# An attention kernel with its softmax maxima taken in pairs, the second layer's first scores moved in front of its values, and the output projections begun in front of the last head's values

## The chip, the cores and the metric

The kernel runs on one core of a Trainium2 chip. The metric is the device time of one execution in microseconds, as the median of several runs. TensorE (PE) multiplies, VectorE (DVE), ScalarE (ACT) and GpSimd (POOL) do the elementwise work, SyncE (SP) issues the loads of weights. Each engine has its own list of instructions, in an order that is fixed when the program is built, and works it off from the top; an instruction may wait on a semaphore for work of another engine, and what stands behind it on that engine waits as well.

## The reference

A diffusion backbone of two layers on 256 latent and 256 context tokens of width 1024, all in f32. Each layer is a half-step SwiGLU block, a token mixer and a second half-step SwiGLU block, each on a normalised and modulated input. The mixer of layer 0 is multi-head latent attention (MLA, 8 heads), for latent and context tokens; that of layer 1 is windowed attention (SWA, 16 query heads on 4 key heads) with a sink logit per head, for the latent tokens alone. In the SWA the latent keys and queries are rotated, the context ones aren't, and one softmax runs over the window, the context and the sink:

```
s_w = jnp.einsum('bkgqd,bkjd->bkgqj', q_rot, k_b).astype(jnp.float32) * scale
s_w = jnp.where(valid, s_w, NEG_INF)
s_c = ctx_scores(q_pl)
...
p_w, p_c, _ = joint_softmax(s_w, s_c, s_s)
return pv('bkgqj,bkjd->bkgqd', p_w, v_b) + pv('bkgqc,bkcd->bkgqd', p_c, v_c)
```

Afterwards all heads' outputs go through one projection (`w_o`) into the residual.

## The kernel before

Every f32 product is done as three matmuls on split operands (high by high, low by high, high by low; lines 210 to 212, `mm3`). A weight tile comes by DMA as `wraw`; ACT casts its high part `whi` (L182), and DVE or POOL subtracts it for the low part `wlo` (L183). Tiles move through rings (`bank` for PSUM, `r2k`, `tmp`, `strip`, `small` for SBUF). A scheduler lays the Python calls out on the engines at build time, so that the order in which the functions are called, together with the rings, decides what stands where.

Both mixers are a pipeline over heads (in the SWA a step is a pair of heads, called head here, so that there are eight). The steps of head h are `project` (its queries, 24 products in the SWA), `rope` (one permutation matmul L739, then POOL L741, DVE L742, POOL L743), `scores` (L769 and mask L774, four score tiles of 128x512), `softmax`, `turn` (16 transposes L787, copies by ACT L792 and DVE L790) and `apply` (probabilities times values, L800, then a split for the projection). The function `pipeline` calls them so that scores run two heads ahead of `turn` and `apply`.

`softmax` is, for each of the four score tiles, on DVE a maximum (L451) and its scaling (L453, with a sink L455), on ACT the exponential with the sum of its row (L457); then for two tiles together the sink's exponential on ACT (L463), its addition and the reciprocal on DVE (L464, L466), and the normalisation, half on DVE (L471) and half on ACT (L469).

In front of the SWA's pipeline stand the projected keys of the latent tokens (copied by ACT, L810, and then rotated), the keys of the context (L819 copies the values, L732 the context keys), and the values of four token blocks. The products of the first queries and keys run while the normalisation of the second stream (ACT L185, L182, L291; DVE L294, L186) is still going on. Behind each pipeline `closing` multiplies by `w_o`, tile by tile: 8 output tiles of 24 products, the i-th three of which need the output of head i.

Of the kernel before, what the change touches and what calls it, by code (L numbers as in the profile page):

```python
# [13 lines left out]
AF = mybir.ActivationFunctionType  # L14
ALU = mybir.AluOpType
AX = mybir.AxisListType

P = 128
# [19 lines left out]
def hybrid_backbone_kernel(ctx, tc, t, out):  # L38
# [6 lines left out]
    def bank(shape=(P, 512)):  # L45
        return ps.tile(list(shape), F32, tag="bank", name="bank")
# [147 lines left out]
    def weight(ap, n=1024, engine=nc.vector, after=None):  # L194
        return weight_split(weight_raw(ap, n), engine, after)
# [59 lines left out]
    class Sublayer:  # L255
# [17 lines left out]
        def place(self, s, k):  # L273
            if k == len(self.hs):
                self.hs.append((r2k(), r2k()))
            return (h[:, SL[s]] for h in self.hs[k])
# [90 lines left out]
    def closing(tiles, chunk, l, streams, nxt, tail, per_tile=0):  # L367


        w = T * len(streams)  # L370
        tail = tail if len(streams) > 1 else 0

        def terms(wt, inputs, cols):
            return [(pair(wt, slice(None), slice(i * P, (i + 1) * P)), pair(x, slice(None), cols)) for i, x in enumerate(inputs)]

        for d in range(KT - tail):
            pump(per_tile)
            ap, inputs = tiles[d]
            wt = weight(ap, len(inputs) * P)
            o = bank()  # L380
            mm3(o[:, :w], terms(wt, inputs, slice(0, w)))
            residual(l, chunk, d, o, streams)
            for s in streams:
                if nxt:
                    nxt.grown(s, d)
        if nxt:
            load_table(AF.Sqrt, nxt.squares[0].last)
        held = [(d, weight(tiles[d][0], len(tiles[d][1]) * P), bank(), tiles[d][1]) for d in range(KT - tail, KT)]
        if nxt:
            nxt.prefetch()  # L390
        for s in streams:
            for d, wt, o, inputs in held:
                mm3(o[:, SL[s]], terms(wt, inputs, SL[s]))
                residual(l, chunk, d, o, (s,))
                if nxt:
                    nxt.grown(s, d)
            if nxt and s in nxt.streams:
                if s == 1:
                    nxt.leading(0)
                last = nxt.stream(s)  # L400
                if nxt.sub == 1 and nxt.l == 1 and s == 1:
                    exp_soon(last)
        if nxt and nxt.streams[-1] in nxt.leads:
            nxt.leading(nxt.streams[-1])
# [40 lines left out]
    def softmax(os, scale, place, sink=None, minus_sink=None):  # L445
# [1 line left out]
        n = len(os)  # L447
        top, sums = small(n), small(n)
        es = []
        for j, (o, w) in enumerate(os):  # L450
            nc.vector.tensor_reduce(top[:, j:j + 1], o[:, :w], axis=AX.X, op=ALU.max)  # L451
            if sink is None:
                nc.vector.tensor_scalar_mul(top[:, j:j + 1], top[:, j:j + 1], -scale)  # L453
            else:
                nc.vector.tensor_scalar(top[:, j:j + 1], top[:, j:j + 1], -scale, minus_sink[:, j // 2:j // 2 + 1], ALU.mult, ALU.min)  # L455
            e = place(j)
            nc.scalar.activation(e, spread(e, o[:, :w]), AF.Exp, bias=top[:, j:j + 1], scale=scale, accum_out=sums[:, j:j + 1])  # L457
            es.append(e)
        for i in range(0, n, 2):
            two = slice(i, i + 2)  # L460
            if sink is not None:
# [61 lines left out]
        nc.scalar.copy(dh[b], dh[a].bitcast(F32))  # L523
        nc.vector.tensor_copy(dl[b], dl[a].bitcast(F32))

    def pipeline(n, project, rope, scores, turn, apply, q, e, at={}, early=False):

        for h in range(n):
            p = turn(*e.pop(0))
            if early and h + 4 < n:  # L530
                q.append(project(h + 4))
            if h + 2 < n:
                e.append(scores(h + 2, *q.pop(0)))
            if h + 3 < n:
                rope(h + 3)
            if h in at:
                at[h]()
            apply(h, *p)
            if not early and h + 4 < n:
                q.append(project(h + 4))  # L540


    def mla_specs():
# [2 lines left out]
    def mla(sl, nxt):  # L546
# [146 lines left out]
        values(0, 0, 2)  # L693
        exp_soon(nq.finish(1))
        values(0, 2, 4)
        q = [project(0)]
        rope(0)
        q.append(project(1))
        e = [scores(0, *q.pop(0))]
        q.append(project(2))  # L700
        e.append(scores(1, *q.pop(0)))
        rope(2)
        q.append(project(3))
        pipeline(MLA_H, project, rope, scores, turn, apply, q, e, {4: lambda: values(1, 0, 4)})
        closing([(t["mwo"][d], O) for d in range(KT)], 5, l, sl.streams, nxt, 2)


    def swa(sl, nxt):
# [94 lines left out]
            split(*oh, o[:, :T])  # L803
            O.append(oh)

        q = [project(0), project(1)]
        plain = []
        for m in range(2):
            p = tmp(T)
            nc.scalar.copy(p, keys(m, 0))  # L810
            plain.append(p)
        values(0, 2)
        for m in range(2):
            K[m] = r2k().bitcast(F32)
# [11 lines left out]
        pipeline(8, project, rope, scores, turn, apply, q, e, early=True)  # L826
        closing([(t["swo"][d], O) for d in range(KT)], 5, l, (0,), nxt, 0)


    def load_tmp(name, n):  # L830
# [176 lines left out]
```

## Time and profile before

| | |
|---|---|
| time, median of 3 runs | 1713.83 us (1713.79 to 1716.16) |
| time of the profiled execution | 1715.96 us |
| its span | 1714.2 us |
| mean granted clock of TensorE | 0.991 |
| busy shares of the span | PE 98%, DVE 60%, ACT 38%, POOL 10% |
| MLA stage (heads and what leads in) | about 475 to 580 us of the span |
| SWA stage | about 1380 to 1480 us of the span |

The profile is one execution. Its busy times are sums over the engine's instructions, the chain is followed back from the last instruction, and a time such as 1386.58 counts from the start of the span. A row of the timeline gives start, duration, engine and line, and in brackets how long the engine had been idle before it, with what it waited for; matmuls overlap, so their durations are longer than their distance.

### The profile page before, as it was taken

The numbers are of one execution on the slowest core, as the hardware profiler recorded it, in microseconds if no ns is written. First come the engines' busy times: TensorE is split into PE (matmuls) and PEld (weight loads), VectorE is DVE, ScalarE is ACT, GpSimd is POOL, SyncE is SP. The second block draws the span as 40 slices with busy tenths as digits, with TensorE's granted clock in tenths as the row PEclk, the third lists the DMA queues.
The fourth block names the chain that finished last, engine by engine and source line by source line (L and its number), as shares of the span: only waits on it lengthen the run. The fifth ranks groups of instructions, "written<-read, shape, count | busy, mean of one in ns | idle before, by whom it ended". The sixth has DMA issues, their size and how long they took to land.

```text
span 1714.2 us, 23757 instructions
## 1 busy us (share of the span) xinstructions
PE 1674.9 (98%) x9448; PEld 1421.5 (83%) x9448; DVE 1029.5 (60%) x1536; ACT 643.9 (38%) x1087; POOL 175.2 (10%) x173
## 2 busy tenths in 40 slices
PE   7999999999999999999999999999999999989997
PEld 4788888888888898888888898888888897789997
DVE  4877477555568567856857465645433467655554
ACT  4432232224456444213222353223222367554443
POOL 1000000004132040000000130000000352110001
PEclk9999999999999999999999999999999999999998
DMA  9556356442211126644645336734332222145553
GB/s 340 174 192 209 112 198 194 138 132 80 87 50 62 47 68 206 202 158 147 208 145 172 111 111 197 240 117 154 104 101 90 93 90 84 60 149 184 172 188 98
DMA packets 72831, 242.71 MB, mean 142 GB/s; under 512 B 8848, under 2 KB 10640, under 8 KB 72720
## 3 DMA queue, kind: packets, MB, share of 16 engines
q1 hardware_dynamic: 72720, 241.20, 43.1%
q8 instruction: 74, 1.21, 0.3%
q14 instruction: 37, 0.30, 0.1%
HBM read 240.11 MB, written 1.05 MB: 141 GB/s over the span
## 4 chain that ended last, share of the span: by engine, by line
PE 90%; DVE 3%; ACT 3%; DMA 2%; issue 2%; POOL 1%; SPq 0%; POOLq 0%; ACTq 0%; DVEq 0%
PE bank L210 28%; PE bank L211 28%; PE bank L212 28%; DMA r2k<-in_modo 1%; PE bank L157 1%; DVE wlo L183 1%; DVE small L451 0%; PE bank L479 0%; ACT whi L182 0%; PE bank L223 0%; PE bank L102 0%; PE bank L800 0%; ACT tmp L457 0%; DVE r2k L294 0%; DMA big<-in_win 0%
## 5 line engine op out<-in xcount | busy, mean ns | idle before, releaser
L210 PE MATMUL bank<-r2k,whi 128*128 128x512 f32 (+1 forms) x2610 | 916.0, 352 | 4.7 <-ACT r2k L185 2.4
L212 PE MATMUL bank<-r2k,wlo 128*128 128x512 f32 (+1 forms) x2610 | 912.0, 350 | 4.3 <-POOL wlo L183 2.2
L211 PE MATMUL bank<-r2k,whi 128*128 128x512 f32 (+1 forms) x2610 | 913.0, 350 | 2.9 <-DVE r2k L186 1.2
L182 ACT CAST whi<-wraw 128x1024 fp32r<-128x1024 f32 (+1 forms) x313 | 321.6, 1028 | 892.0 <-PE bank L211 537.7
L210 PEld LDWEIGHTS bank<-r2k,whi 128*128 128x128 f32 x2610 | 493.5, 190 | 84.1 <-ACT whi L182 9.2
L212 PEld LDWEIGHTS bank<-r2k,wlo 128*128 128x128 f32 x2610 | 495.1, 190 | 69.7 <-POOL wlo L183 3.1
L211 PEld LDWEIGHTS bank<-r2k,whi 128*128 128x128 f32 x2610 | 495.2, 190 | 68.2 <-DVE r2k L186 1.9
L183 DVE TENSOR_TENSOR wlo<-wraw,whi 128x1024 fp32r<-128x1024 f32 (+1 forms) x302 | 363.6, 1206 | 145.5 <-ACT whi L182 138.8
L151 DVE SCALAR_TENSOR_TENSOR big<-modraw,conds,big 128x1024 f32<-128x1024 f32 x196 | 242.4, 1279 | 12.4 <-DMA modraw<-in_modw 11.9
L248 POOL TENSOR_TENSOR strip<-strip 128x256 f32<-128x256 f32 x64 | 65.7, 1040 | 1319.9 <-issue 657.5
L364 DVE SCALAR_TENSOR_TENSOR x<-bank,mod,x 128x256 f32<-128x256 f32 x192 | 86.1, 480 | 181.9 <-PE bank L212 181.9
L425 DVE TENSOR_TENSOR tmp<-bank,tmp 128x512 f32<-128x512 f32 (+1 forms) x88 | 54.9, 624 | 179.9 <-PE bank L212 178.0
L183 DVE TENSOR_TENSOR r2k<-tmp,r2k 128x512 fp32r<-128x512 f32 (+1 forms) x88 | 54.4, 618 | 1.5 <-ACT r2k L182 1.4
L182 ACT CAST r2k<-tmp 128x512 fp32r<-128x512 f32 (+1 forms) x88 | 49.7, 566 | 10.8 <-DVE tmp L425 10.5
L183 DVE TENSOR_TENSOR r2k<-bank,r2k 128x512 fp32r<-128x512 f32 (+2 forms) x73 | 40.7, 593 | 17.5 <-ACT r2k L182 17.1
L423 ACT ACTIVATE tmp<-bank 128x512 f32<-128x512 f32 (+1 forms) x88 | 47.3, 537 | 7.4 <-PE bank L212 7.4
L451 DVE TENSOR_REDUCE small<-bank 128x1 f32<-128x512 f32 (+1 forms) x64 | 37.0, 614 | 7.4 <-PE bank L774 7.2
L182 ACT CAST r2k<-bank 128x512 fp32r<-128x512 f32 (+2 forms) x73 | 34.4, 524 | 14.2 <-PE bank L212 8.8
L242 ACT ACTIVATE strip<-x 128x256 f32<-128x256 f32 x80 | 30.6, 410 | 17.8 <-DVE x L364 17.0
L186 DVE SCALAR_TENSOR_TENSOR r2k<-r2k,mod 128x256 fp32r<-128x256 f32 x45 | 29.3, 674 | 8.4 <-ACT r2k L185 7.9
L457 ACT ACTIVATE tmp<-bank,small 128x512 f32<-128x512 f32 x32 | 21.8, 687 | 24.8 <-DVE small L453 14.6
L104 DVE TENSOR_TENSOR mod<-bank,c_modb 128x4 f32<-128x4 f32 x56 | 5.3, 154 | 37.2 <-PE bank L102 37.2
(156 smaller groups left out, 933.1 us busy)
## 6 DMA issues: line engine op xcount, KB each, us to landing
wraw<-in_win SPq DMA_DIRECT2D x172, 512.0 KB, 3.5
modraw<-in_modw SPq DMA_DIRECT2D x128, 512.0 KB, 4.2
wraw<-in_wout SPq DMA_DIRECT2D x64, 448.0 KB, 3.3
wraw<-in_wout SPq DMA_DIRECT2D x32, 512.0 KB, 3.8
r2k<-in_modo SPq DMA_DIRECT2D x32, 256.0 KB, 5.8
wraw<-in_mwo SPq DMA_DIRECT2D x8, 512.0 KB, 3.5
wraw<-in_swq SPq DMA_DIRECT2D x8, 512.0 KB, 3.4
wraw<-in_swo SPq DMA_DIRECT2D x8, 512.0 KB, 3.5
```

The costliest lines, as they stand in the source:

```text
L151: nc.vector.scalar_tensor_tensor(acc[s], raw, conds[:, kt, s:s + 1], acc[s], ALU.mult, ALU.add)
L182: nc.scalar.copy(hi, src)
L183: return engine.tensor_tensor(lo, src, hi.bitcast(F32), ALU.subtract)
L210: nc.tensor.matmul(o, lhsT=ah, rhs=bh, start=(i == 0), stop=False)
L211: nc.tensor.matmul(o, lhsT=ah, rhs=bl, start=False, stop=False)
L212: nc.tensor.matmul(o, lhsT=al, rhs=bh, start=False, stop=(i == n - 1))
L242: nc.scalar.activation(q, x, AF.Square)
L248: nc.gpsimd.tensor_tensor(self.parts[0], self.parts[0], q, ALU.add)
L364: nc.vector.scalar_tensor_tensor(xs[d][:, SL[s]], o[:, SL[s]], mod[l][:, s, c:c + 1], xs[d][:, SL[s]], ALU.mult, ALU.add)
L423: nc.scalar.activation(sg[:, :w], og[:, :w], AF.Silu)
L425: nc.vector.tensor_tensor(pr[:, :w], ou[:, :w], sg[:, :w], ALU.mult)
L451: nc.vector.tensor_reduce(top[:, j:j + 1], o[:, :w], axis=AX.X, op=ALU.max)
```

## The change

Four edits. In `softmax` the maxima of two tiles are taken one after the other, and one scaling instruction serves both; the two exponentials follow. In front of the MLA pipeline the second and third head's queries are projected earlier than before. In front of the SWA pipeline the rotated keys and the context keys come before all values, the first head's scores follow the first block of values, and the second head's scores come before the last block. And `opening` begins the output projection behind the last head's `turn` and in front of its `apply`: with the inputs of all heads but the last, one output tile in the MLA (21 products of 128x512), two in the SWA (42 products of 128x256). `closing` then does what remains of these tiles.

```diff
+    def opening(aps, n, inputs, w):
+        begun = []
+        for ap in aps:
+            begun.append((weight(ap, n * P), bank()))
+            for i, x in enumerate(inputs):
+                products(begun[-1], n, i, x, w)
+        return begun, len(inputs)
+
+    def products(tile, n, i, x, w):
+        (wh, wl), o = tile
+        a, cols = slice(i * P, (i + 1) * P), slice(0, w)
+        nc.tensor.matmul(o[:, :w], lhsT=wh[:, a], rhs=x[0][:, cols], start=(i == 0), stop=False)
+        nc.tensor.matmul(o[:, :w], lhsT=wh[:, a], rhs=x[1][:, cols], start=False, stop=False)
+        nc.tensor.matmul(o[:, :w], lhsT=wl[:, a], rhs=x[0][:, cols], start=False, stop=(i == n - 1))
...
@@ closing
-            wt = weight(ap, len(inputs) * P)
-            o = bank()
-            mm3(o[:, :w], terms(wt, inputs, slice(0, w)))
+            begun, i0 = opened
+            if d < len(begun):
+                o = begun[d][1]
+                for i in range(i0, len(inputs)):
+                    products(begun[d], len(inputs), i, inputs[i], w)
+            else:
+                wt = weight(ap, len(inputs) * P)
+                o = bank()
+                mm3(o[:, :w], terms(wt, inputs, slice(0, w)))
...
@@ softmax
-        for j, (o, w) in enumerate(os):
-            nc.vector.tensor_reduce(top[:, j:j + 1], o[:, :w], axis=AX.X, op=ALU.max)
+        for i in range(0, n, 2):
+            for j in (i, i + 1):
+                o, w = os[j]
+                nc.vector.tensor_reduce(top[:, j:j + 1], o[:, :w], axis=AX.X, op=ALU.max)
+            two = top[:, i:i + 2]
...
+                nc.vector.tensor_scalar(two, two, -scale, minus_sink[:, i // 2:i // 2 + 1], ALU.mult, ALU.min)
+            for j in (i, i + 1):
+                o, w = os[j]
+                e = place(j)
+                nc.scalar.activation(e, spread(e, o[:, :w]), AF.Exp, bias=top[:, j:j + 1], scale=scale, accum_out=sums[:, j:j + 1])
...
@@ pipeline
+            if h == n - 1:
+                opened = before_last()
             apply(h, *p)
...
@@ mla
-        q = [project(0)]
+        q = [project(0), project(1)]
         rope(0)
-        q.append(project(1))
+        q.append(project(2))
         e = [scores(0, *q.pop(0))]
-        q.append(project(2))
         e.append(scores(1, *q.pop(0)))
...
@@ swa
-        q = [project(0), project(1)]
+        q = [project(0)]
...
+        q.append(project(1))
-        values(0, 2)
         for m in range(2):
             K[m] = r2k().bitcast(F32)
             roped(K[m][:, X], plain[m])
         rope(0)
-        rope(1)
         for m in range(2):
             nc.scalar.copy(K[m][:, C], keys(m, 1))
+        values(0, 1)
+        e = [scores(0, *q.pop(0))]
+        rope(1)
+        values(1, 3)
         q.append(project(2))
-        e = [scores(0, *q.pop(0))]
-        values(2, 4)
         e.append(scores(1, *q.pop(0)))
+        values(3, 4)
```

Where the instructions stand is seen on each engine's list. First place: the start of the SWA on PE, where the last products of the latent keys end. Before (`bank<-whi,r2k` and `bank<-wlo,r2k` are the products of the values, 48 of them, L739 the permutations of the rotation):

```order
L211 MATMUL bank<-r2k,whi 128x256
L212 MATMUL bank<-r2k,wlo 128x256
L210 MATMUL bank<-whi,r2k 128x256
L211 MATMUL bank<-wlo,r2k 128x256
L212 MATMUL bank<-whi,r2k 128x256
...
L739 MATMUL bank<-tmp,permr 128x256 x2
L739 MATMUL bank<-r2k,permr 128x256 x2
L210 MATMUL bank<-r2k,whi 128x256
```

The same place now, where L769 is the permutation and the products behind it are those of the context's keys:

```order
L210 MATMUL bank<-r2k,whi 128x256
L211 MATMUL bank<-r2k,whi 128x256
L212 MATMUL bank<-r2k,wlo 128x256
L769 MATMUL bank<-tmp,permr 128x256 x2
L769 MATMUL bank<-r2k,permr 128x256
L210 MATMUL bank<-r2k,whi 128x256
L211 MATMUL bank<-r2k,whi 128x256
```

The permutations have moved from behind the 48 value products to directly behind the keys' own products. What they read is copied by ACT (L810 before, L840 now), whose list there has changed little. Now it reads:

```order
L291 ACTIVATE r2k<-r2k,mod_91,coefA_93 128x256
L185 ACTIVATE r2k<-r2k,mod_91 128x256
L182 CAST r2k<-r2k 128x256
L785 COPY r2k<-bank 128x256
L840 COPY tmp<-bank 128x256 x2
L785 COPY r2k<-bank 128x256
```

The copies stand, as before, behind the whole normalisation (L185, L182, L291) of the second stream; only the second of the two L785 copies went behind them.

Second place: one head of the SWA pipeline on DVE, from the split of a weight in front of it. Before:

```order
L183 TENSOR_TENSOR wlo<-wraw,whi 128x1024
L451 TENSOR_REDUCE small<-bank 128x1 x2
L455 TENSOR_SCALAR small<-small,minus_sink 128x1 x2
L451 TENSOR_REDUCE small<-bank 128x1 x2
L455 TENSOR_SCALAR small<-small,minus_sink 128x1 x2
L742 TENSOR_TENSOR strip<-bank,c_ropeS 128x256
L464 TENSOR_TENSOR small<-small 128x2
L183 TENSOR_TENSOR r2k<-bank,r2k 128x256
L466 RECIPROCAL small<-small 128x2
L471 TENSOR_SCALAR x<-x,small 128x2x256
L790 COPY r2k<-bank 128x512
L464 TENSOR_TENSOR small<-small 128x2
```

The same head now:

```order
L183 TENSOR_TENSOR wlo<-wraw,whi 128x1024
L475 TENSOR_REDUCE small<-bank 128x1 x3
L480 TENSOR_SCALAR small<-small,minus_sink 128x2
L475 TENSOR_REDUCE small<-bank 128x1
L772 TENSOR_TENSOR strip<-bank,c_ropeS 128x256
L480 TENSOR_SCALAR small<-small,minus_sink 128x2
L491 TENSOR_TENSOR small<-small 128x2
L493 RECIPROCAL small<-small 128x2
L183 TENSOR_TENSOR r2k<-bank,r2k 128x256
L498 TENSOR_SCALAR x<-x,small 128x2x256
L491 TENSOR_TENSOR small<-small 128x2
L820 COPY r2k<-bank 128x512
```

Three maxima instead of two now stand in front of the first scaling, and so in front of the first exponential. On ACT a head was laid out so before, from the cast of a weight:

```order
L182 CAST whi<-wraw 128x1024
L457 ACTIVATE tmp,small<-bank,small 128x512 x2
L463 ACTIVATE small<-small,c_sink 128x2
L182 CAST r2k<-bank 128x256
L457 ACTIVATE tmp,small<-bank,small 128x512 x2
L469 ACTIVATE tmp<-tmp,small 128x512
L463 ACTIVATE small<-small,c_sink 128x2
L792 COPY r2k<-bank 128x512 x2
L469 ACTIVATE tmp<-tmp,small 128x512
```

and stands so now:

```order
L182 CAST whi<-wraw 128x1024
L484 ACTIVATE tmp,small<-bank,small 128x512 x4
L490 ACTIVATE small<-small,c_sink 128x2
L182 CAST r2k<-bank 128x256
L490 ACTIVATE small<-small,c_sink 128x2
L496 ACTIVATE tmp<-tmp,small 128x512
L822 COPY r2k<-bank 128x512 x2
L496 ACTIVATE tmp<-tmp,small 128x512
```

All four exponentials come first, and the two sink exponentials (L463 before, L490 now), for which DVE's sums wait, stand behind them.

Third place: the end of the SWA on PE. Before, with L800 the applies of heads 6 and 7, L787 the turn of head 7 and L210 the first product of the projection:

```order
L787 MATMUL bank<-c_ident,x 128x128 x16
L800 MATMUL bank<-r2k 64x256
L787 MATMUL bank<-c_ident,tmp 128x128
L800 MATMUL bank<-r2k 64x256 x7
L787 MATMUL bank<-c_ident,tmp 128x128 x15
L800 MATMUL bank<-r2k 64x256 x8
L210 MATMUL bank<-r2k,whi 128x256
```

Now, with L830 the applies, L817 the turns and L379 to L381 the products of `opening`, of which 42 stand at the "...":

```order
L817 MATMUL bank<-c_ident,x 128x128 x16
L830 MATMUL bank<-r2k 64x256 x8
L817 MATMUL bank<-c_ident,tmp 128x128 x16
L379 MATMUL bank<-r2k,whi 128x256
L380 MATMUL bank<-r2k,whi 128x256
L381 MATMUL bank<-r2k,wlo 128x256
...
L830 MATMUL bank<-r2k 64x256 x8
L210 MATMUL bank<-r2k,whi 128x256
```

The opened products stand between the last turn and the last apply; the apply of head 6 keeps its place between the two turns.

## Rows read from the trace of the kernel before

**Rows 1.** Page, part 4: the chain that ended last, by engine.
```profile
PE 90%; DVE 3%; ACT 3%; DMA 2%; issue 2%; POOL 1%; SPq 0%; POOLq 0%; ACTq 0%; DVEq 0%
```

**Rows 2.** Windows: busy us (instructions) of PE, PEld, DVE, ACT, POOL; granted clock; DMA.
```profile
1384.00:1388.00 4.00, 2.94 (x25) 2.73 (x24) 4.00 (x6) 4.00 (x13) 2.50 (x3) 1.00 0.11 32
...
1430.00:1440.00 10.00, 10.00 (x84) 7.98 (x84) 7.46 (x19) 7.33 (x19) 1.48 (x2) 1.00 0.15 54
1472.00:1474.00 2.00, 2.00 (x13) 1.11 (x13) 0.43 (x1) 0.73 (x2) 0.00 (x0) 0.68 0.03 8
1474.00:1476.00 2.00, 2.00 (x9) 0.86 (x6) 0.00 (x0) 0.16 (x1) 0.00 (x0) 0.50 0.00 0
```

**Rows 3.** Timeline of PE at the start of the SWA: start, us, instruction, idle before.
```profile
1383.80 0.28 PE L210 MATMUL bank<-whi,r2k 128*128 128x256 f32 x1
...
1386.58 0.39 PE L211 MATMUL bank<-wlo,r2k 128*128 128x256 f32 x1 [1.06 <-DVE wlo L183]
```

**Rows 4.** Timeline of ACT at the same place.
```profile
1386.88 0.40 ACT L182 CAST r2k<-r2k 128x256 fp32r<-128x256 f32 x1
1387.18 0.64 ACT L755 COPY r2k<-bank 128x256 f32<-128x256 f32 x2
1387.70 0.64 ACT L810 COPY tmp<-bank 128x256 f32<-128x256 f32 x2
```

**Rows 5.** Chain through the SWA's heads: start, us, engine and line.
```profile
1420.72 2.43 DVE wlo L183
1423.14 1.20 DVE small L451 x2
...
1430.53 0.95 ACT whi L182
1431.51 1.23 DVE wlo L183
...
1451.93 1.20 DVE small L451 x2
...
1458.77 1.20 DVE small L451 x2
...
1462.11 0.42 DVE r2k L183
...
1464.41 0.60 DVE r2k L790
1465.12 0.49 DVE x L471
1465.61 1.20 DVE small L451 x2
...
1471.05 0.48 ACT r2k L792
```

**Rows 6.** Timeline of ACT: the first exponentials of the third head.
```profile
1424.56 0.69 ACT L457 ACTIVATE x<-bank,small 128x512 f32<-128x512 f32 x1 [3.60 <-DVE small L455]
...
1425.24 0.68 ACT L457 ACTIVATE x<-bank,small 128x512 f32<-128x512 f32 x1
...
1425.90 0.29 ACT L463 ACTIVATE small<-small,c_sink 128x2 f32<-128x2 f32 x1
```

**Rows 7.** Timeline of PE: mask of the third head's scores, apply of head 6.
```profile
1421.53 0.40 PE L774 MATMUL bank<-band,ident 128*128 128x128 bf16 x4
...
1471.58 0.65 PE L800 MATMUL bank<-r2k 128*64 128x256 f32 x2 [2.51 <-ACT r2k L792]
```

**Rows 8.** Waits of PE: line, for what, us in total, times, longest.
```profile
PE bank L211 <- DVE r2k L183: 1.2, 2, 0.9
...
PE bank L497 <- DVE big L516: 0.9, 1, 0.9
...
PE bank L651 <- POOL big L516: 0.4, 1, 0.4
```

**Rows 9.** Timeline of POOL at the start of the MLA.
```profile
483.31 2.40 POOL L183 TENSOR_TENSOR wlo<-wraw,whi 128x1024 fp32r<-128x1024 f32 x1
```

More of the change, by code (lines that the diff above doesn't have):

```diff
@@ L365, in residual, with closing @@
                                            ALU.mult, ALU.add)
-    def closing(tiles, chunk, l, streams, nxt, tail, per_tile=0):
+    def opening(aps, n, inputs, w):
[11 more added lines that the diff above has]
+        nc.tensor.matmul(o[:, :w], lhsT=wl[:, a], rhs=x[0][:, cols], start=False, stop=(i == n - 1))
+    def closing(tiles, chunk, l, streams, nxt, tail, per_tile=0, opened=((), 0)):
         w = T * len(streams)
@@ L449, in softmax @@
         es = []
-        for j, (o, w) in enumerate(os):
-            nc.vector.tensor_reduce(top[:, j:j + 1], o[:, :w], axis=AX.X, op=ALU.max)
+        for i in range(0, n, 2):
[3 more added lines that the diff above has]
+            two = top[:, i:i + 2]
             if sink is None:
-                nc.vector.tensor_scalar_mul(top[:, j:j + 1], top[:, j:j + 1], -scale)
+                nc.vector.tensor_scalar_mul(two, two, -scale)
             else:
[L455 to L458, printed above, removed]
+                nc.vector.tensor_scalar(two, two, -scale, minus_sink[:, i // 2:i // 2 + 1], ALU.mult, ALU.min)
[3 more added lines that the diff above has]
+                nc.scalar.activation(e, spread(e, o[:, :w]), AF.Exp, bias=top[:, j:j + 1], scale=scale, accum_out=sums[:, j:j + 1])
+                es.append(e)
         for i in range(0, n, 2):
@@ L524, in doubled, with pipeline @@
         nc.vector.tensor_copy(dl[b], dl[a].bitcast(F32))
-    def pipeline(n, project, rope, scores, turn, apply, q, e, at={}, early=False):
+    def pipeline(n, project, rope, scores, turn, apply, q, e, at={}, early=False, before_last=None):
         for h in range(n):
@@ L540, in pipeline @@
                 q.append(project(h + 4))
+        return opened
     def mla_specs():
@@ L703, in mla @@
         q.append(project(3))
-        pipeline(MLA_H, project, rope, scores, turn, apply, q, e, {4: lambda: values(1, 0, 4)})
-        closing([(t["mwo"][d], O) for d in range(KT)], 5, l, sl.streams, nxt, 2)
+        opened = pipeline(MLA_H, project, rope, scores, turn, apply, q, e, {4: lambda: values(1, 0, 4)},
+                          before_last=lambda: opening([t["mwo"][0]], KT, O, TT))
+        closing([(t["mwo"][d], O) for d in range(KT)], 5, l, sl.streams, nxt, 2, opened=opened)
     def swa(sl, nxt):
@@ L816, in swa @@
         rope(0)
-        rope(1)
         for m in range(2):
             nc.scalar.copy(K[m][:, C], keys(m, 1))
+        values(0, 1)
+        e = [scores(0, *q.pop(0))]
+        rope(1)
+        values(1, 3)
         q.append(project(2))
-        e = [scores(0, *q.pop(0))]
-        values(2, 4)
         e.append(scores(1, *q.pop(0)))
+        values(3, 4)
         rope(2)
         q.append(project(3))
-        pipeline(8, project, rope, scores, turn, apply, q, e, early=True)
-        closing([(t["swo"][d], O) for d in range(KT)], 5, l, (0,), nxt, 0)
+        opened = pipeline(8, project, rope, scores, turn, apply, q, e, early=True,
+                          before_last=lambda: opening([t["swo"][d] for d in range(2)], KT, O, T))
+        closing([(t["swo"][d], O) for d in range(KT)], 5, l, (0,), nxt, 0, opened=opened)
     def load_tmp(name, n):
```

## The prediction

> **What bounds the kernel now.** I read the chain of the page first: 90% of the span is TensorE, so the kernel as a whole is its products, and the change removes none [rows 1]. It can only add or remove time where PE waits, which is where other engines set the pace; so I went to PE's waits and then stage by stage. Three places matter.
>
> At the start of the SWA, PE ends the latent keys and begins the value products at 1383.80; it waits once, 1.06 us, for a weight split on DVE [rows 3]. ACT and DVE are busy without a break there (4.00 of 4.00 us) and the clock stays at full speed, 2.4 GHz [rows 2].
>
> In the heads of the SWA the chain runs through ACT and DVE from one head's maxima to the next: 1423.14 and 1451.93 are the third and the sixth head's, three rounds of 9.6 us; then 1458.77 and 1465.61, rounds of 6.84 us without a weight split [rows 5]. PE shows no idle time in 1430 to 1440 [rows 2], so it is not far behind that pace; but the next head's maxima wait for the split on DVE (1431.51), this for the cast on ACT (1430.53), and this for all that stands before it on ACT [rows 5].
>
> At the end PE waits 2.51 us for the copies of head 6's transposes [rows 7], and afterwards runs at a granted clock of 0.68 and 0.50, that is for a time at the lower level, 1.2 GHz [rows 2]. In the MLA the waits are short: 0.9 and 0.4 us at its start, and two for a split, 1.2 us together [rows 8].
>
> **The start of the SWA.** The permutations of the rotated keys now stand where the value products stood. They read copies that ACT makes behind the second stream's normalisation. This ends with the cast at 1386.88, one L755 copy follows at 1387.18, and two take 0.52 until L810 at 1387.70 [rows 4]; so the first key copy can start at 1387.18 + 0.26 = 1387.44 and, at 0.38 for one (0.64 less 0.26), end at 1387.8. The 48 value products hid this. With 24 of them behind the first scores and 24 further on, PE has nothing to do from 1383.80 to 1387.8: 4.0 us, of which the 1.06 us wait of before goes, net +3.0. The clock: before the apply at 1471.58 an idle stretch of 2.51 us was followed by 2 us at 0.68 and 2 us at 0.50 [rows 2, 7], which lost 2 x 0.32 + 2 x 0.50 = 1.6 us; the wait of 1.06 us lost nothing [rows 2, 3]. At 4.0 us I count the loss in: +1.6. Against this stands slack: the third head's mask ends at 1421.53 + 0.40 = 1421.93 [rows 7], its maxima begin at 1423.14, behind two splits of together 2.43 us on DVE [rows 5], of which the new list has one on DVE and the others on POOL. So the first 1.2 us are absorbed: 3.0 + 1.6 - 1.2 = **+3.4**. Bounds: +1.8 if the clock holds, +4.6 if the splits move along and nothing is absorbed.
>
> The rule that this rests on is that an engine doesn't take an instruction past a waiting one; the trace shows it in L810, whose bank PE had finished before 1383.80 and which runs at 1387.70 [rows 3, 4]. The Trainium skill says it too (TensorE: Matmul & The Clock Gate, Architectural detail): the lists of ScalarE and VectorE are strictly first in, first out; the trace agrees.
>
> **The paired scaling.** It saves one small DVE instruction per pair of tiles, and puts a third maximum in front of the first exponential: 1.20 / 2 = 0.60 us [rows 5]. Before, the first exponential starts 1424.56 - 1423.14 = 1.42 us behind the first maximum [rows 5, 6]; now 2.02. ACT's sum up to the next cast is the same set of instructions, and from 1424.56 to 1430.53 it has no pause in the chain, so the cast, the split and the next maxima come 0.6 us later in each round: 9.6 becomes 10.2. Three such rounds: +1.8.
>
> In the two rounds without a split (6.84 us) DVE itself is the gate. Before, the first sink exponential (0.29 us) came after two exponentials of 0.68 [rows 6], and DVE did the first half of its sums, split and normalisation while ACT did the other two. Now it comes after four, at 2.02 + 4 x 0.68 = 4.74, and ends at about 4.95. Behind it DVE has the split (0.42), two copies of 0.60, two normalisations of 0.49 [rows 5] and four small instructions, which I estimate at 0.1 each: 3.0 us, so the next maxima come at 7.95 less what overlaps, some 7.85 instead of 6.84. Two such rounds: +2.0. Together **+3.8**; bounds 0, if all of it were slack, and +4.5, if each of the three rounds gives 0.15 and each of the last two 0.1 more.
>
> What hid these delays before would have to be PE's own pace of 9.6 us; it still takes that, and the longer chain is now 10.2, so there is no cover. The Trainium skill has a rule for each side (Perfetto Trace Analysis, Optimizing Scalar/DVE Operations): grouping pays if the engine is saturated, at about 60 ns of access saved per DVE instruction on SBUF; if it isn't but causes gaps elsewhere, breaking work up lets it finish sooner. DVE is busy 7.46 of 10 us in this stretch [rows 2], so the second sentence would be the one that holds, and it speaks against the edit; by the first alone the SWA's eight heads would gain an estimated 8 x 2 x 0.06 = 1 us.
>
> **The opening.** In the SWA it stands behind the last turn. The large wait, 2.51 us, is in front of the apply of head 6, which keeps its place between the turns; nothing new stands in front of it. Its copies by ACT now come ahead of the last head's normalisation: counted from that head's first maximum, the four exponentials end at 4.74, one sink exponential follows, the first copy (0.48) ends at about 5.45 instead of 1471.05 + 0.48 - 1465.61 = 5.92 [rows 5]: **-0.5**. The half clock behind the wait stays. Bounds: 0, and -4.1 if the whole wait and its clock loss went (2.51 + 1.6).
>
> **The MLA.** At its start the waits of 0.9 and 0.4 us for the rotated queries [rows 8] lie behind other products now and go. But the third head's queries need a low part that POOL makes in 2.40 us [rows 9], behind the same rotation's instructions on POOL; their products now stand in front of the first scores, where before they stood behind them. The new wait lies between 0 and 2.40; from 20 products between the permutation and the first use I take 1.6, so +0.3 net (bounds -1.3 and +1.1). At the end the opening covers the smaller of the two waits for the split (1.2 - 0.9 = 0.3) [rows 8], and the later exponentials lengthen the larger one by some 0.2: -0.1. Together **+0.2**.
>
> **The sum.** 3.4 + 3.8 - 0.5 + 0.2 = +6.9 us: 1722.9 for an execution like the profiled one (1715.96), which lay 2.1 above the median of the runs. Against the median, 1713.83, it is 1720.7.
>
> **The rivals.** *Faster: the heads go by PE's pace and the hole at the end closes.* If the earlier scores put the softmax so far ahead that its longer round is never waited for, the +3.8 is nothing, the copies for head 6 are there in time, and 4.1 us go at the end; MLA -1.3 - 0.3; the start still +1.8 with a steady clock. Sum -3.9: 1709.9. For it speaks that PE has no idle time in 1430 to 1440; against it that the third head's maxima begin later and not sooner, and that each round's cast stands behind its own head's exponentials. It decides if the round on ACT and DVE stays under PE's 9.6 us.
> *No change: the start alone counts.* The paired scaling's delay lies in slack, the start gives +1.8 to +3.4, the end -0.5, the MLA nothing: +2 on average, 1715.9. For it: a wait inside the chain that I take for work. Against it: the rows of ACT follow each other without one.
> *Slower still: the clock falls at more places.* The rounds without a split hold 1 us more of idle time each, and the MLA's new wait can reach 2.4 us, near the 2.51 that cost 1.6. One or two more such losses, and the start without absorption: 6.9 + 1.6 + 1.2 = +9.7 or more, 1723.5 to 1726.
>
> **How the numbers follow.** The forecast 0.47, the faster rival 0.15, no change 0.20, slower still 0.18. The predicted time is the forecast's, 1720.7; its own range is 1717.5 to 1723.5. The range leaves out the lower half of the faster rival and the upper half of the slowest: 1710.5 to 1725. A measurement of this kernel can tell about 0.2%, 3.4 us: faster than 1710.4 is the first rival, 0.15; within 1710.4 to 1717.3 the second, 0.20; slower the rest, 0.65.
>
> **What would show it.** In the changed profile: PE idle for about 4 us in front of the first permutation (L769), with ACT's L840 as the releaser, and a granted clock under 1 behind it; rounds from maximum to maximum (L475) of 10.2 and 7.85 us; a wait of about 2.5 us or more in front of the apply of head 6 and none in front of head 7's; at the MLA's start a wait for a POOL split in place of two for rotated queries. The prediction is wrong if ACT reaches the key copies earlier than I read, if the rounds stay at 9.6, or if the wait in front of head 6's apply is gone.

## The result and the profile after

The change makes the kernel slower: 1722.72 us (median of 4 runs, 1721.47 to 1723.15) against 1714.38 us for the kernel before on the same chip. The ratio is 1.0044, with a 95% interval of 1.0032 to 1.0057, that is +8.3 us on the medians. The forecast was +6.9 us, 1720.7, with a range of 1710.5 to 1725.0; it counted from 1713.83, the median of the kernel before without its fourth run. All medians here and below leave out two slow runs, one of e1_single_scaling and one of g2_opening_alone, at granted clocks of 0.84 and 0.56.

The page of the changed kernel, parts 1 and 4 (busy us, share of the span and instructions of PE; the chain by engine):

```profile
PE 1675.4 (97%) x9448; PEld 1422.6 (83%) x9448; DVE 1028.0 (60%) x1504; ACT 644.1 (37%) x1087; POOL 176.6 (10%) x173
...
PE 89%; ACT 3%; DVE 3%; issue 2%; POOL 1%; DMA 1%; SPq 0%; POOLq 0%; ACTq 0%; DVEq 0%
```

TensorE does the same 9448 matmuls, DVE 1504 instructions where it had 1536, and the span is longer (1719.7 against 1714.2 us). To see where, the two spans are cut at matmuls that both kernels have and that the change doesn't move: the transposes of the norms (L229) in front of the MLA, behind it, in front of the SWA and behind it. Timeline of PE, the kernel before:

```profile
469.22 0.38 PE L229 MATMUL bank<-c_ident,small 128*128 128x128 f32 x2
...
619.92 0.43 PE L229 MATMUL bank<-c_ident,small 128*128 128x128 f32 x2
...
1379.38 0.38 PE L229 MATMUL bank<-c_ident,small 128*128 128x128 f32 x2
...
1506.42 0.43 PE L229 MATMUL bank<-c_ident,small 128*128 128x128 f32 x2 [1.04 <-DVE small L226]
```

and the changed one:

```profile
467.51 0.38 PE L229 MATMUL bank<-c_ident,small 128*128 128x128 f32 x2
...
620.63 0.43 PE L229 MATMUL bank<-c_ident,small 128*128 128x128 f32 x2
...
1380.13 0.38 PE L229 MATMUL bank<-c_ident,small 128*128 128x128 f32 x2
...
1512.06 0.69 PE L229 MATMUL bank<-c_ident,small 128*128 128x128 f32 x2 [1.04 <-DVE small L226]
```

The MLA's stretch went from 150.70 to 153.12 us (+2.42), the SWA's from 127.04 to 131.93 (+4.89); the stretch between them stayed at 759.5. What lies in front of 469 us the change doesn't touch; it came out at 467.1 to 469.2 in the profiles of this study. What lies behind takes 207.8 us in the kernel before and 207.6 in the changed one; the row at 1512.06 is longer because the clock falls once more there, as it does in the kernel before just behind its row. So two profiles are compared stage by stage below, and not by their spans.

**The start of the SWA.** Timelines of PE and of ACT, changed kernel:

```profile
1388.61 1.64 PE L769 MATMUL bank<-tmp,permr 128*128 128x256 f32 x4 [3.90 <-ACT tmp L840]
```
```profile
1387.63 0.39 ACT L182 CAST r2k<-r2k 128x256 fp32r<-128x256 f32 x1
1387.92 0.37 ACT L785 COPY r2k<-bank 128x256 f32<-128x256 f32 x1
1388.19 0.64 ACT L840 COPY tmp<-bank 128x256 f32<-128x256 f32 x2
```

PE waits 3.90 us for the copy of the first keys, and ACT makes it behind the last cast of the second stream and one other copy; before there was one wait of 1.06 us [rows 3, 4]. The windows (columns as in [rows 2]) show the clock in three places, at the end of the MLA, behind this wait, and at the end of the SWA:

```profile
572.00:574.00 2.00, 1.65 (x11) 1.65 (x12) 1.49 (x3) 0.04 (x1) 0.00 (x0) 0.83 0.00 0
574.00:576.00 2.00, 2.00 (x11) 2.00 (x11) 0.42 (x1) 0.74 (x2) 0.00 (x0) 0.50 0.00 0
576.00:578.00 2.00, 2.00 (x14) 1.91 (x13) 1.32 (x3) 1.47 (x4) 0.00 (x0) 0.82 0.00 0
...
1388.00:1390.00 2.00, 1.39 (x4) 1.16 (x5) 2.00 (x4) 1.09 (x5) 1.90 (x3) 0.77 0.76 248
1390.00:1392.00 2.00, 2.00 (x9) 1.78 (x8) 1.35 (x4) 0.00 (x0) 2.00 (x3) 0.50 0.04 14
1392.00:1394.00 2.00, 2.00 (x16) 2.00 (x16) 0.00 (x0) 0.00 (x0) 2.00 (x4) 0.87 0.00 0
...
1480.00:1482.00 2.00, 2.00 (x17) 1.18 (x16) 0.93 (x4) 1.48 (x3) 0.00 (x0) 1.00 0.03 8
```

Each of the first two groups lost 2 x (0.17 + 0.50 + 0.18) = 1.7 us or 2 x (0.23 + 0.50 + 0.13) = 1.7 us at the lower level, 1.2 GHz. Behind the wait at the end of the SWA the clock stayed at 2.4 GHz, where before it fell [rows 2].

**The heads of the SWA.** The chain, changed kernel, from the third head's maxima to the eighth's:

```profile
1424.83 1.05 ACT whi L182
1425.90 1.23 DVE wlo L183
1427.14 1.80 DVE small L475 x3
...
1429.47 2.79 ACT x L484 x8
...
1437.70 1.80 DVE small L475 x3
...
1447.96 1.80 DVE small L475 x3
...
1458.22 1.27 DVE small L475 x3
...
1466.05 1.27 DVE small L475 x3
...
1473.88 1.79 DVE small L475 x3
```

The rounds are 10.56, 10.26, 10.26, 7.83 and 7.83 us, where they were 9.6 three times and 6.84 twice [rows 5]. PE now waits inside three of them, in the middle of a head's turn, 0.65 us each time for an exponential:

```profile
1440.56 1.09 PE L817 MATMUL bank<-c_ident,x 128*128 128x128 f32 x8 [0.65 <-ACT tmp L484]
```

**The ends.** PE in the MLA (its start and its end) and at the end of the SWA, changed kernel:

```profile
483.81 0.50 PE L212 MATMUL bank<-r2k,wlo 128*128 128x512 f32 x1 [1.69 <-POOL wlo L183]
...
500.70 0.39 PE L681 MATMUL bank<-r2k,big 128*128 128x256 f32 x1 [0.71 <-POOL big L543]
...
571.12 0.38 PE L210 MATMUL bank<-r2k 128*128 128x256 f32 x1 [0.94 <-ACT r2k L182]
...
572.35 0.39 PE L211 MATMUL bank<-r2k 128*128 128x256 f32 x1 [0.85 <-DVE r2k L183]
...
1479.35 2.43 PE L830 MATMUL bank<-r2k 128*64 128x256 f32 x16 [2.01 <-ACT r2k L822]
...
1488.62 1.95 PE L830 MATMUL bank<-r2k 128*64 128x256 f32 x16
```

The same place at the end of the MLA in the kernel before, where the clock stayed at 2.4 GHz (1.00 from 570 to 578 us):

```profile
571.35 0.38 PE L210 MATMUL bank<-r2k 128*128 128x256 f32 x1 [0.58 <-ACT r2k L182]
...
572.59 0.38 PE L211 MATMUL bank<-r2k 128*128 128x256 f32 x1 [0.86 <-DVE r2k L183]
```

In the SWA the wait in front of head 6's apply is still there, 2.01 for 2.51 us [rows 7], shorter than the 2.5 us or more that the prediction gave as a sign, and the opened products stand behind it, in front of head 7's apply at 1488.62, which has no wait. At the start of the MLA the waits of 0.9 and 0.4 us [rows 8] are replaced by one of 1.69 for a split on POOL and, further on, one of 0.71 for the next rotation.

The SWA's stretch in three parts, each a difference of rows above (L229 in front; maxima of the third head; maxima of the eighth head; L229 behind):

| us | to the third head's maxima | five rounds | to the next L229 |
|---|---|---|---|
| before | 43.76 | 42.47 | 40.81 |
| changed | 47.01 | 46.74 | 38.18 |
| difference | +3.25 | +4.27 | -2.63 |

### The profile page after: what moved, and what is told of

Read it like the earlier page. It is cut to its first block, busy times and chain, and to the rows that moved or that the text cites. A ratio compares the mean times of both kernels' runs of the same rounds, so it can differ in the third digit from the quotient of the medians.

```text
span 1719.7 us, 23706 instructions
## 1 busy us (share of the span) xinstructions
PE 1675.4 (97%) x9448; PEld 1422.6 (83%) x9448; DVE 1028.0 (60%) x1504; ACT 644.1 (37%) x1087; POOL 176.6 (10%) x173
## 4 chain that ended last, share of the span: by engine, by line
PE 89%; ACT 3%; DVE 3%; issue 2%; POOL 1%; DMA 1%; SPq 0%; POOLq 0%; ACTq 0%; DVEq 0%
PE bank L210 28%; PE bank L211 28%; PE bank L212 28%; PE bank L157 1%; DVE small L475 1%; ACT tmp L484 1%; DMA r2k<-in_modo 1%; POOL wlo L183 1%; ACT x L484 0%; PE bank L506 0%; ACT whi L182 0%; PE bank L223 0%; DVE wlo L183 0%; PE bank L102 0%; DMA big<-in_win 0%
## 5 line engine op out<-in xcount | busy, mean ns | idle before, releaser
L210 PE MATMUL bank<-r2k,whi 128*128 128x512 f32 (+1 forms) x2586 | 908.4, 353 | 4.5 <-ACT r2k L185 2.4
L182 ACT CAST whi<-wraw 128x1024 fp32r<-128x1024 f32 (+1 forms) x313 | 321.5, 1028 | 878.5 <-PE bank L211 521.6
L210 PEld LDWEIGHTS bank<-r2k,whi 128*128 128x128 f32 x2586 | 489.1, 190 | 83.9 <-ACT whi L182 9.2
L182 ACT CAST r2k<-tmp 128x512 fp32r<-128x512 f32 (+1 forms) x88 | 49.7, 566 | 10.1 <-DVE tmp L447 9.8
L182 ACT CAST r2k<-bank 128x512 fp32r<-128x512 f32 (+2 forms) x73 | 34.8, 525 | 28.0 <-PE bank L212 18.7
L183 POOL TENSOR_TENSOR wlo<-wraw,whi 128x1024 fp32r<-128x1024 f32 x11 | 27.1, 2480 | 13.5 <-ACT whi L182 13.3
```

The source lines that it names most:

```text
L182: nc.scalar.copy(hi, src)
L183: return engine.tensor_tensor(lo, src, hi.bitcast(F32), ALU.subtract)
L210: nc.tensor.matmul(o, lhsT=ah, rhs=bh, start=(i == 0), stop=False)
```

## The experiments

All times are medians beside runs of the kernel before on the same chip, with the ratio to these and its 95% interval. The kernel before has medians of 1714.38 to 1715.40 in these sets, so that a difference of about 1 us between two sets tells nothing; there the stretches of the profiles, one execution each, carry the argument. They are taken between the same matmuls as above.

**Undo the softmax edit alone.** (e1_single_scaling)

```diff
-            two = top[:, i:i + 2]
...
-                nc.vector.tensor_scalar(two, two, -scale, minus_sink[:, i // 2:i // 2 + 1], ALU.mult, ALU.min)
...
+                nc.vector.tensor_scalar(top[:, j:j + 1], top[:, j:j + 1], -scale, minus_sink[:, j // 2:j // 2 + 1], ALU.mult, ALU.min)
```

> The changed kernel with only the softmax edit undone: each maximum is scaled by itself again. Theory (the third maximum in front of the first exponential lengthens each round, the start of the stage is another matter): the rounds between the third and the eighth head's maxima go back from 10.26 and 7.83 us to 9.6 and 6.84 us, 4 us less; at the end the apply of head 6 again comes 5.97 us behind its maxima in place of 5.47, and may bring a half clock back (1.6), so 1718 to 1721 us against 1722.7. Rival (the new order of the start, not the scaling, makes the rounds long): rounds stay at 10.2 and 7.8, time stays within 1 us of 1722.7.

Measured 1718.23 us, ratio 1.0020 (1.0011 to 1.0029), 4.5 less than the change. Its chain:

```profile
1418.29 2.40 POOL wlo L183
...
1420.71 3.39 DMA wraw<-in_swo
...
1424.20 1.05 ACT whi L182
...
1425.28 1.84 DVE wlo L183
1427.12 1.20 DVE small L473 x2
...
1436.71 1.20 DVE small L473 x2
...
1462.75 1.20 DVE small L473 x2
...
1469.59 1.20 DVE small L473 x2
```

The rounds are exactly those of before (9.59 and 6.84, five rounds 42.47), in the new order of the start: the theory holds, the rival falls. Two things were not expected. The third head's maxima come 49.13 us behind the norm's transposes, later than in the change (47.01): a weight load (3.39 us) waits for its buffer until POOL has made a low part, and the cast waits for the load. And the first layer's stretch is 150.17 us, not 153.12. So the time lies in the expected range by two things that cancel: the shorter rounds are mostly eaten up in front of them and behind them (the SWA's stretch is 130.54 us, only 1.39 less), and most of the gain, 2.95 us, comes from the MLA, which the expectation left out.

**The softmax edit alone on the kernel before.** (e2_paired_only)

```diff
-            nc.vector.tensor_reduce(top[:, j:j + 1], o[:, :w], axis=AX.X, op=ALU.max)
...
+            for j in (i, i + 1):
+                o, w = os[j]
+                nc.vector.tensor_reduce(top[:, j:j + 1], o[:, :w], axis=AX.X, op=ALU.max)
+            two = top[:, i:i + 2]
...
+                nc.vector.tensor_scalar(two, two, -scale, minus_sink[:, i // 2:i // 2 + 1], ALU.mult, ALU.min)
```

> The kernel before with the softmax edit alone: maxima of two tiles scaled together. Theory: rounds of 10.2 and 7.8 us in place of 9.6 and 6.84, +4 us up to the eighth head's maxima, of which the end gives 0.5 to 2 us back: 1716.5 to 1718.5 against 1714.4. Rival (in the old order the delay lies in slack): within 1 us of 1714.4.

Measured 1721.14 us, ratio 1.0038 (1.0026 to 1.0051): +6.4, and the expectation of 1716.5 to 1718.5 was missed on the high side. The stretches give the parts: MLA +1.96, SWA +4.68. In the MLA the two waits at the end are 0.94 and 0.85 us, followed by granted clocks of 0.68 and 0.50; I had left the MLA out. In the SWA the third head's maxima come 2.4 us later, in the old order, the five rounds take 4.66 more, and the rest up to the next norm 2.4 less.

**Undo the start of the SWA alone.** (e3_start_undone)

```diff
-        q = [project(0)]
+        q = [project(0), project(1)]
...
+        values(0, 2)
         for m in range(2):
             K[m] = r2k().bitcast(F32)
...
-        values(0, 1)
         e = [scores(0, *q.pop(0))]
-        rope(1)
-        values(1, 3)
+        values(2, 4)
```

> The changed kernel with only the start of the second layer's attention put back: two blocks of values in front of the rotations, scores behind. Theory: PE's wait of 3.9 us for the key copies and the half clock behind it go, the wait of 1.06 us for the split comes back, the third head's maxima come 3 us sooner, the rounds stay at 10.2 and 7.8: 1719 to 1720.5 against 1722.7. Rival (the third head's maxima are held by the weight split in any order, so that the wait at the start is absorbed): within 1 us of 1722.7.

Measured 1721.95 us, ratio 1.0040 (1.0026 to 1.0053): 0.8 less than the change, which can't be told from it, where 2 to 3.5 were expected; the rival's time came out. The chain shows why, and PE's timeline and the clock in its window show what follows:

```profile
1425.09 2.27 DVE wlo L183
1427.36 1.80 DVE small L475 x3
```
```profile
1430.22 1.45 PE L817 MATMUL bank<-c_ident,tmp 128*128 128x128 f32 x8 [3.08 <-ACT x L484]
```
```profile
1430.00:1432.00 2.00, 1.78 (x11) 1.79 (x12) 0.35 (x2) 2.00 (x8) 0.73 (x1) 0.70 0.35 141
1432.00:1434.00 2.00, 2.00 (x11) 2.00 (x11) 1.58 (x6) 1.97 (x8) 0.00 (x0) 0.50 0.00 0
```

The wait of 3.9 us for the keys is gone (1.06 as before), and the third head's scores end 4.4 us sooner than in the change. But its maxima come 46.16 us behind the norm, only 0.85 sooner: they stand behind the weight split on DVE, as the rival said, and this behind a weight's cast on ACT, which follows the second head's normalisation. With the pairing that cast begins 2.39 us later behind the norm than in the kernel before, and the maxima come 2.40 later. Behind the late maxima PE waits 3.08 us for the third head's exponential, with the same loss of clock. So the rival's mechanism holds in the old order; in the order of the next run the same split comes 2.5 us sooner.

**The new start with two blocks of values in front of the rotations.** (c1_values_first)

```diff
         q.append(project(1))
+        values(0, 2)
         for m in range(2):
             K[m] = r2k().bitcast(F32)
...
-        values(0, 1)
         e = [scores(0, *q.pop(0))]
         rope(1)
-        values(1, 3)
+        values(2, 3)
```

> The changed kernel with two blocks of values called in front of the rotations again, everything else as changed (the first scores still in front of the third block). Theory (the value products hid ACT's copies of the keys): PE's wait of 3.9 us shrinks to about 1 us, no half clock there; but with the pairing the heads pause elsewhere by up to 3 us, as they do in the old order, so the gain is 0 to 3 us: 1719.5 to 1722.5. Rival (the copies are late in any order): wait of 3.9 us and 1722.7.

Measured 1718.94 us, ratio 1.0025 (1.0015 to 1.0035), 3.8 less than the change and a little under the expected 1719.5 to 1722.5. PE's one wait there is 1.06 us again, the clock stays at 1.00, and the third head's maxima come 43.70 us behind the norm, as in the kernel before (43.76); the five rounds are 46.75. With the cover back, the earlier scores cost nothing here, and of the 3.08 us wait of the old order 0.95 is left. In the new order it is the 48 products missing in front of the permutations that make the third head's maxima late: putting them back gains 3.3 us there.

**Pair the maxima in the SWA only.** (e5_paired_second_layer; without a sink the softmax is that of before)

```diff
-        for i in range(0, n, 2):
+        for j, (o, w) in enumerate(os if sink is None else ()):
+            nc.vector.tensor_reduce(top[:, j:j + 1], o[:, :w], axis=AX.X, op=ALU.max)
+            nc.vector.tensor_scalar_mul(top[:, j:j + 1], top[:, j:j + 1], -scale)
...
+        for i in range(0, n if sink is not None else 0, 2):
```

> The changed kernel with the softmax of the first layer as before; the maxima are paired in the second layer alone. Theory (in the first layer pairing lengthens two waits at the end from 1.44 to 1.79 us, the clock falls behind them, 1.7 us, and one new wait of 0.7 us appears at the start): the first layer's stage is 2.8 us shorter, the second's unchanged: 1719.5 to 1721 against 1722.7. Rival (the first layer is bound by PE and does not feel the pairing): within 1 us of 1722.7.

Measured 1721.10 us, ratio 1.0037 (1.0025 to 1.0049), 1.6 less than the change by the medians, just above the expected 1719.5 to 1721. The MLA's stretch is 150.20 us, 2.92 less, as expected: the waits at its end are 0.55 and 0.85 us, no half clock follows, and the wait of 0.71 us at its start is gone. What the MLA's new start is worth by itself can be read here too: nothing, 150.20 us with it, and 150.13 in g2 below, which also scales singly and has the opening there, but the old start. The SWA's is 1.86 longer (133.79): here the clock fell behind the wait of 2.01 us at its end (0.62 and 0.53), where in the change it didn't.

**No opening.** (e4_no_opening: the products of both projections all stand in `closing` again)

```diff
-                          before_last=lambda: opening([t["mwo"][0]], KT, O, TT))
+                          before_last=lambda: ((), 0))
...
-                          before_last=lambda: opening([t["swo"][d] for d in range(2)], KT, O, T))
+                          before_last=lambda: ((), 0))
```

> The changed kernel without the opening of the output projections, in both layers. Theory (the opening stands behind the large wait and covers only the small one in front of the last apply): the waits in front of the last applies come back, 0.3 us in the first layer and up to 0.7 in the second: 1722.5 to 1724. Rival (the opening is what shortened the end by 2.6 us): 1725 or more.

Measured 1723.45 us, ratio 1.0048 (1.0036 to 1.0061): 0.7 more than the change, no difference that can be told. The MLA's stretch is 0.6 longer, with a wait of 0.34 us in front of its last apply again; the SWA's is 1.49 longer, but its start lost 3.4 us to the clock where the change lost 1.7. From the apply of head 6 to the next norm, the part in which the opening stands, it is only 0.27 us longer. So the rival, by which the opening shortened the end by 2.6 us, falls.

**The opening alone, and the opening one head sooner.** (g2_opening_alone, g1_opening_earlier, both on the kernel before)

```diff
-            if h == n - 1:
+            if h == n - 2:
                 opened = before_last()
```

> The kernel before with the opening alone, where the change puts it, in front of the last head's apply. Theory: it covers the wait of 0.34 us in the first layer and up to 0.3 in the second, the waits of 1.4 and 2.51 us in front of the apply before it stay: 1713.5 to 1714.8 against 1714.8. Rival (the opening is worth several us wherever it stands): 1712 or less.

> The kernel before with the opening alone, called one head sooner: in front of the apply of the last head but one, with the outputs of six heads (18 products of 128x512 in the first layer, 36 of 128x256 in the second). Theory (the large wait lies in front of that apply): the 36 products, 4.3 us, fill the wait of 2.51 us, no half clock follows it, the waits of 0.58 and 0.86 us in the first layer go as well: 1709 to 1711.5 against 1714.8. Rival (the end goes by the softmax of the last head, whatever stands on PE): 1713.5 to 1715.

Where the change puts it, the opening alone measured 1713.68 us, ratio 0.9994 (0.9985 to 1.0002): no difference that can be told; the MLA's stretch is 0.57 us shorter, the SWA's 0.24. One head sooner it measured 1707.41 us, ratio 0.9958 (0.9946 to 0.9970): 8.0 us faster than before, more than expected (1709 to 1711.5). Its PE at the end of the SWA:

```profile
1463.10 1.97 PE L813 MATMUL bank<-c_ident,x 128*128 128x128 f32 x16
1464.82 0.36 PE L379 MATMUL bank<-r2k,whi 128*128 128x256 f32 x1
...
1469.30 1.95 PE L826 MATMUL bank<-r2k 128*64 128x256 f32 x16
1471.18 1.97 PE L813 MATMUL bank<-c_ident,tmp 128*128 128x128 f32 x16
1473.08 2.25 PE L826 MATMUL bank<-r2k 128*64 128x256 f32 x16
1475.25 0.39 PE L379 MATMUL bank<-r2k,whi 128*128 128x256 f32 x1
```

From the turn at 1463.10 to the end of the last apply no row has a wait. The SWA's stretch is 4.87 us shorter: 2.51 of the wait, 1.7 of the clock, and 0.6 more that I don't trace. The MLA's is 2.37 shorter: 0.58, 0.86 and 0.34 us of waits are 1.8 of it.

**The whole change with the opening one head sooner.** (h2_change_opening_sooner; the last diff on the changed kernel)

> The whole change, with the opening called one head sooner. Theory: the wait of 2.01 us in front of the apply of head 6 goes and the projection's products fill it; in the first layer the waits of 0.94 and 0.85 us and the half clock behind them (1.7) go: 5 to 7 us less, 1715.5 to 1718. Rival (with the pairing the end goes by the last head's softmax, so the products only move): 1720.5 to 1722.7.

Measured 1716.58 us, ratio 1.0011 (1.0002 to 1.0020), 6.1 less than the change: MLA -3.66, SWA -2.29. By the stretches, one head sooner is worth 6.0 us here and 6.4 on the kernel before (g1 against g2): here 3.7 of it in the MLA, where a half clock goes with the waits, there 4.6 in the SWA, where it goes. The rest of the change still costs about 8 us (h2 against g1: 8.6; the change against g2: 8.1).

**A candidate for the best of both.** (h1_sooner_values_first: the kernel of g1, that is the kernel before with the sooner opening, and in the SWA the start of c1; the MLA's start is that of before)

> The kernel before with the opening one head sooner, and with the second layer's start in the new order except that two blocks of values still stand in front of the rotations; each maximum is scaled by itself. Theory (the new order of the scores costs nothing once the key copies are covered, but with single scaling the heads had no wait there to lose): the same as with the sooner opening alone, 1706.5 to 1708.5. Rival (the first scores in front of the third block bring the softmax of the third head forward, as it did with the pairing, by up to 2.8 us): 1704.5 to 1706.

Measured 1708.42 us, ratio 0.9963 (0.9951 to 0.9976). The rival falls: nothing is gained over the sooner opening alone (1707.41). By the stretches a little is lost: the third head's maxima come 0.98 us later than in g1, and the SWA's stretch is 0.98 longer, 123.15 for 122.17 us. So the new order of the scores pays only with the paired maxima. The fastest version of the study is the kernel before with the sooner opening and nothing else of the change, though the medians of g1 and h1 alone don't tell them apart.

## Why the prediction was right

The direction, the size and the places of the loss were forecast, and the terms for the start and the rounds came out. Two other terms were mis-sized, the end of the SWA by -2.1 us and the MLA by +2.2; that they cancel is luck.

- *The start of the SWA: +3.4 forecast, +3.25 measured.* The wait was 3.90 us for 4.0, ACT's L840 its releaser, and the clock fell for 1.7 us as counted in. The absorption of 1.2 us came too: the first turn stands 1420.25 - 1380.13 = 40.12 us behind the norm in the changed kernel and 1415.06 - 1379.38 = 35.68 before, 4.44 later, the maxima 3.25. But its reason was misread. The 2.43 us of [rows 5] are one split and not two, where such a split took 1.23 us in the rounds; it runs beside a split on POOL, in the kernel before:

```profile
1419.70 2.36 POOL L183 TENSOR_TENSOR wlo<-wraw,whi 128x1024 fp32r<-128x1024 f32 x1 [1.79 <-ACT whi L182]
```

  In the changed kernel the one split in front of the third head's maxima took 1.23 us (1425.90), and the scores' last mask ended level with it, so all slack was used up. That the number fits is luck. One reading of the order was off too, without a consequence: 24 of the value products stand in front of the first scores and not behind them, but behind the permutations all the same. That the 48 value products were the cover is shown by c1.
- *The rounds: +3.8 forecast, +4.27 measured.* That ACT and DVE, not PE, set the rounds is shown by e1, where they go back to the old ones to 0.01 us. The rounds without a split were 7.83 for 7.85. Of those with one the second and third took 0.66 more, for 0.60; the first took 0.96, since its first exponential came 2.33 us behind its maxima and not 2.02. The working has a slip that changed little: 4.74 and a sink exponential of 0.29 are 5.03, not 4.95.
- *The end of the SWA: -0.5 forecast, -2.63 measured.* The step "the half clock behind the wait stays" failed. The apply of head 6 came at 5.47 us behind the last maxima, as forecast (5.45), which is the -0.5; but the clock stayed up, and that is 1.7 us. The opening gave 0.3 more, by g2 and e4. The clock isn't a property of the change: behind 2.51 us it fell in the kernel before and in g2 and not in e1, behind 2.01 us it fell in e5 and not in the change, e2, e3, e4 and c1. What decides there stays open.
- *The MLA: +0.2 forecast, +2.42 measured.* The size of this term was wrong. The later exponentials lengthened a wait at the end, as forecast, but not the one named: that of 0.86 us for the split stayed (0.85), and one of 0.58 us for ACT's cast in front of it, which isn't among [rows 8], became 0.94. A half clock followed, 1.7 us, that I had not put anywhere outside the slower rival. It followed these two waits in all five kernels profiled with paired maxima in the MLA and the opening in its place or absent (changed, e2, e3, e4, c1), and in none of the four with 0.53 to 0.59 and 0.86 (before, e1, g2, e5). At the start the split on POOL cost 1.69 us for the 1.6 taken. The 0.71 us wait for the next rotation was not foreseen; it is there in the kernels with the pairing and the MLA's new start and gone with single scaling (e1, e5). The opening gave 0.6.
- *The sum.* 3.25 + 4.27 - 2.63 + 2.42 = 7.3 us; the medians say 8.3. The profiled execution is the fastest of the four timed (1721.47), and that of before (1715.96) lies above three of its four; the remaining 1 us lies in executions that no trace shows.
- *What the sum left out: the edits don't add.* It takes the start and the pairing as two prices. The SWA's stretch, with the opening in its place in all four, says otherwise: 126.80 us with neither (g2), 130.54 with the new start alone (e1), 131.47 with the pairing alone (e3), 131.93 with both. Alone they cost 3.7 and 4.7 us, together 5.1 (the half clock at the end, 1.7 us, is in g2's time alone, so without it they overlap still more). The terms above are right as places of the changed kernel, but undoing one edit doesn't give its term back: the third head's maxima wait for the scores, which the new start delays, and for the weight split, which the pairing delays, so that without the new start they come only 0.85 us sooner (e3).
- *The opening.* That it covers only small waits in front of the last apply is shown by e4 and g2, and that the waits in front of the apply before it were the ones to cover by g1 and h2.
- *The rivals.* The faster one needed rounds at PE's pace; the rounds are those of ACT and DVE. "No change" needed slack for the pairing; e2 shows there is none, in either layer. Of the slower one a part came true: one more loss of clock, in the MLA.

## What to carry to other kernels

Two matters decide what an instruction ahead of a chain costs: not its own duration alone, but how many rounds it lengthens, and what waits at the end of each. A wait is covered by work that stands in front of the instruction that waits; work one instruction behind it, as the opening here, covers next to nothing (g2: no difference that can be told), and the same kind of products one head sooner made the kernel 8 us faster. Before products are moved, look for what they hide: the 48 value products hid a queue on ACT, and with them back the new order cost nothing there (with single scaling, h1, it still cost 1 us). And where two edits delay the same instruction, the price of both is not the sum: the two edits of the SWA cost 3.7 and 4.7 us alone and 5.1 together.

## What the runs showed of the hardware

A wait can cost as much again in clock. Behind the wait of 3.9 us at the start of the SWA the granted clock fell to the lower level in every profile that had it (changed, e1, e4, e5, h2), which cost 1.7 us in four of them and 3.4 in e4; behind the wait of 3.08 us in e2 and e3 it cost 1.7 too. At the end of the MLA two waits with one product between them, together 1.79 to 1.82 us, were followed by the lower level in each of five profiles, and two of together 1.39 to 1.44 us in none of four. At the end of the SWA a wait of 2.51 us was followed by it in two of three profiles and one of 2.01 us in one of six, so a forecast there can be no better than about 1.7 us either way.

A weight split on DVE (128x1024) took 1.23 us in the rounds. In front of the third head's maxima, where POOL was making a split of the same shape when it began, it took 2.43 us before, 2.27 in e2 and e3 and 1.84 in e1, and ended about 1.1 us behind the end of POOL's split each time. That POOL's split held it is read from these rows alone; no run takes it away.
